# A two-layer decoder trunk on one core: where the down-projection writes four of its norms and one of its weight differences

## The chip, the core and the metric

The kernel runs on one core of a Trainium2 chip. The metric is the device time of one execution in microseconds (us). The engines of the core are TensorE (PE in the profile, PEld for its weight loads), VectorE (DVE), ScalarE (ACT), GpSimd (POOL) and SyncE (SP, which here only issues DMAs). The kernel before takes 2775.11 us, the median of three runs (2769.86 to 2777.68).

## The reference, cut to what matters

The trunk has two layers (DEPTH = 2) on 1024 tokens of 1024 features, all in float32. What concerns the change is the end of each layer, where `h = silu(a) * b` has 2816 features:

```
ffn = jnp.einsum('bsf,fd->bsd', jax.nn.silu(a) * b, w_down)
return layer_norm(ALPHA * x + ffn, ln2_g, ln2_b)
```

The layer norm takes mean and variance over the 1024 features of a token, divides by `sqrt(var + 1e-5)`, multiplies by the gain `g` and adds `b`.

## The kernel before, in words

**Products.** A float32 product is made of three matmuls (lines 110 to 112): each operand is split into a high part (ScalarE, line 90) and the rest (VectorE or GpSimd, line 94), and high x high, high x low and low x high are summed in one PSUM bank. `split` takes an engine for the second part; `L94` in a row is thus the second half of a split, on DVE or on POOL.

**Down-projection.** `down` (line 834 on) uses a 2x2 block scheme with seven products in place of eight. In the order of `plan` they are A11, A12, S2, S1, S4, S3, A22, numbered n = 0 to 6 in the code; the text calls them the first to the seventh product. Each is a sum over 11 steps j (two of the 22 blocks of 128 features per step). In a step, `operands` loads a block of `h` from DRAM (line 860) and up to two 128x512 blocks of `w_down`, forms a sum or difference of weights, and splits block and weights into 128x1024 parts; then PE does four quarters q (one PSUM bank each), three matmuls a quarter, so 12 matmuls a step. Four PSUM banks (`bank_a`) hold one set of sums and four (`bank_x`) another. After a product's last step, `add` (lines 903 to 907) adds banks to the rows `y` of the result, 128 tokens each: tiles 0, 2, 4, 6 are complete after the fifth product, tiles 1, 3, 5, 7 after the seventh. The last six steps of the seventh product (eight in the last layer, `LATE`) have operands in buffers of their own, and PE does them quarter by quarter, so that each quarter's tile can be finished while PE does the next (line 933 on).

**Differences of the weights.** The weight operand of the first product is a block itself; that of S2, S1, S3 and A22 is a difference that GpSimd makes. In the third product (S2, lines 872 to 881) a step loads the block of `h`, `w1[:, hi]` and `w0[:, hi]`; GpSimd makes T2 (line 880), which this step's split needs at once, and T3 (line 881), which is kept in `kept` and needed only by the sixth product (S3). In the fourth product (S1) GpSimd makes one more difference a step (line 888), needed by the seventh. The fifth product (S4, line 889) needs no difference: its step loads `h` and `w1[:, hi]`, and one instruction of 1024 columns splits them. `e_lo` (line 893) gives the second half of the splits of the odd steps of the sixth product to GpSimd, all others to VectorE.

**Norms.** `finish` (line 958) norms a finished tile: statistics of two halves (`bn_stats`, line 259), aggregation (267), a square root on ScalarE (269), reciprocal and a correction of it (271 to 277, instructions of one column), `(z - mean) * g` on VectorE (290), the multiplication by the reciprocal root on ScalarE (291), and the addition of `b` (292), on GpSimd in the first layer and on VectorE in the last. It also appends a piece of work to `pend`: in the first layer the transposition of the tile for the next layer (`to_first`: eight transposes on PE, line 298, then splits), in the last the store of the tile to the output (line 971, issued by SP). `pending()` takes one piece off that list. The even tiles are finished right behind the fifth product.

**Order.** SP and PE run their instructions in the order in which the program writes them. On VectorE, ScalarE and GpSimd a list scheduler of the compiler sets the order at build time: of what is ready by its own clock it takes the instruction of highest priority, which is the one written first, unless a block raises the priority (`urgent`, `high_priority`). On the chip every engine then works strictly in that order. In the text each load stands directly ahead of its use; SP runs ahead of that as far as free buffers let it: the raw blocks go in turn to tags `ws` (3 buffers), `X` (14, shared with what is kept) and `s` (3), the split operands to `w` (6 buffers, two a step, so three steps).

Of the kernel before, what the change touches and what calls it, by code (L numbers as in the profile page):

```python
# [15 lines left out]
ALU = mybir.AluOpType  # L16
# [44 lines left out]
class Trunk:  # L61
# [772 lines left out]
    def down(self, l):  # L834


        nc = self.nc
        last = l + 1 == DEPTH
        wd = self.ins["w_down"]
        lo, hi = slice(0, HALF), slice(HALF, 1024)  # L840
        bank_a = [self.bank() for _ in range(4)]
        bank_x = [self.bank() for _ in range(4)]
        kept, t2 = [None] * NJ, [None] * NJ
        y, half = [None] * 8, [None] * 4
        stages = itertools.cycle(("ws", "X", "s"))
        first = itertools.cycle(("ws", "X", "ws"))

        def operands(n, name, j, late):

            st = self.new([P, 1024], F32, next(first if n == 0 else stages))  # L850
            if late or (n == 0 and j < 4):
                both = self.new([P, 2, 1024], F32R, "X")
                wh, wl = both[:, 0, :], both[:, 1, :]
            else:
                wh, wl = self.new([P, 1024], F32R, "w")[:], self.new([P, 1024], F32R, "w")[:]
            hs = st[:, lo]
            if name == "A11":
                b1 = self.new([P, HALF], F32, "s")
                hs = b1[:]
            nc.sync.dma_start(hs, self.hs[STATIONARY.index(name), j])  # L860
            w0, w1 = wd[l, 2 * j], wd[l, 2 * j + 1]
            other = None
            if name == "A11":

                nc.sync.dma_start(st[:], w0)
                if j % 2 == 0:
                    kept[j] = self.new([P, 2, 2, HALF], F32, "X")
                nc.gpsimd.tensor_tensor(kept[j - j % 2][:, j % 2, 0, :], st[:, hi], st[:, lo], op=ALU.subtract)
                other = st[:, lo]
            elif name == "A12":  # L870
                nc.sync.dma_start(st[:, hi], w1[:, lo])
            elif name == "S2":

                k = kept[j - j % 2][:, j % 2]
                nc.sync.dma_start(st[:, hi], w1[:, hi])
                nc.sync.dma_start(k[:, 1, :], w0[:, hi])
                if j % 4 == 0:
                    t2[j] = self.new([P, 4, HALF], F32, "X")
                other = t2[j - j % 4][:, j % 4]
                nc.gpsimd.tensor_tensor(other, st[:, hi], k[:, 0, :], op=ALU.subtract)  # L880
                nc.gpsimd.tensor_tensor(k[:, 1, :], st[:, hi], k[:, 1, :], op=ALU.subtract)
            elif name in ("S1", "S3"):
                other = kept[j - j % 2][:, j % 2, int(name == "S3"), :]
                if name == "S1":

                    t4 = t2[j - j % 4][:, j % 4]
                    nc.sync.dma_start(st[:, hi], w1[:, lo])
                    nc.gpsimd.tensor_tensor(t4, t4, st[:, hi], op=ALU.subtract)
            elif name == "S4":
                nc.sync.dma_start(st[:, hi], w1[:, hi])  # L890
            else:
                other = t2[j - j % 4][:, j % 4]
            e_lo = "gpsimd" if n == 5 and j % 2 else "vector"
            if other is None:
                self.split(wh, wl, st[:], "scalar", e_lo)
            else:
                self.split(wh[:, lo], wl[:, lo], hs, "scalar", e_lo)
                self.split(wh[:, hi], wl[:, hi], other, "scalar", e_lo)
            return wh, wl

        def add(q, odd, cs, ps, first, op):
            z = y[2 * q + odd][:, cs]
            with self.urgent():
                if first:
                    nc.vector.scalar_tensor_tensor(z, z, ALPHA, ps, op0=ALU.mult, op1=op)  # L905
                else:
                    nc.vector.tensor_tensor(z, z, ps, op=op)

        def step(banks, q, ops, first, end):
            wh, wl = ops  # L910
            ts = slice(q * P, (q + 1) * P)
            self.product(banks[q][:], [(wh[:, ts], wl[:, ts], wh[:, hi], wl[:, hi])], first, end, True)


        plan = [
            ("A11", bank_a, True, False, []),
            ("A12", bank_x, True, True, [(0, lo, False, ALU.add)]),
            ("S2", bank_a, False, False, [(0, hi, True, ALU.add)]),
            ("S1", bank_x, True, False, [(1, hi, True, ALU.add)]),
            ("S4", bank_x, False, True, [(0, hi, False, ALU.add)]),  # L920
            ("S3", bank_a, False, True, [(1, hi, False, ALU.add), (1, lo, True, ALU.add)]),
            ("A22", bank_a, True, True, [(1, lo, False, ALU.subtract)]),
        ]
        for n, (name, banks, fresh, closes, reads) in enumerate(plan):
            if n == 4:
                g, b = self.gains(l, 1)
            held = []
            for j in range(NJ):
                if n == 0 and j == 3:
                    self.flush(True)  # L930
                if not last and (n, j) in ((5, 6), (5, 9), (6, 1), (6, 3)) or last and n == 6 and j in (1, 2, 3, 4):
                    self.pending()
                late = n == 6 and j >= NJ - (LATE if last else 6)
                ops = operands(n, name, j, late)
                if late:
                    held.append((j, ops))
                    continue
                for q in range(4):
                    step(banks, q, ops, fresh and j == 0, closes and j == NJ - 1)
                if n == 1 and j < 8:  # L940
                    y[j] = self.new([P, D], F32, "pt" if j in (0, 1, 2) else "q" if j == 3 else "t")
                    nc.sync.dma_start(y[j][:], self.spill1[j])
                if n == 1 and j == 9:
                    for q in range(4):
                        add(q, 0, lo, bank_a[q][:], True, ALU.add)
            for q in range(4):
                for j, ops in held:
                    step(banks, q, ops, False, j == NJ - 1)
                for odd, cs, first, op in reads:
                    add(q, odd, cs, banks[q][:], first, op)  # L950
                if n == 4:
                    self.finish(l, 2 * q, y, g, b)
                elif n == 5:
                    half[q] = self.stats(y[2 * q + 1], (1,))
                elif n == 6:
                    self.finish(l, 2 * q + 1, y, g, b, self.stats(y[2 * q + 1], (0,), half[q]))
# [144 lines left out]
```

## Time and profile before

| | |
|---|---|
| median of three runs | 2775.11 us (2769.86 to 2777.68) |
| profiled execution | 2775.4 us, span 2773.4 us |
| mean granted TensorE clock | 0.971 |
| busy, share of the span | PE 93%, PEld 76%, DVE 69%, ACT 44%, POOL 53% |
| DMA | 140 GB/s over the span, HBM read 281.75 MB, written 104.43 MB |

The profiled execution's own time is 2.0 us over its span. Matmuls are pipelined: the duration of one in a row is longer than the distance to the next, so steps are read from start times. Idle time in square brackets is that of the engine just before the instruction, with what ended it.

### The profile page before, as it was taken

Reading aid. Unit: us, or ns where it says so; the run is one execution under the profiler, and the core shown is the slowest. Engines: PE = TensorE matmul, PEld = TensorE weight load, DVE = VectorE, ACT = ScalarE, POOL = GpSimd, SP = SyncE. Lnnn points to the kernel's source line nnn. Section 1 sums busy time; section 2 is a strip of 40 time slices with the busy share of each in tenths; the row PEclk is TensorE's granted clock in tenths of the full one; section 3 lists DMA queues with packets and bytes.
Section 4 is the critical chain, followed back from the end, with each engine's and each line's share of the span. In section 5 each row is a group of like instructions: output and inputs, shape, how many; then the busy total and the mean of one; then the engine's idle time right before and its main releaser. Section 6 shows DMA issues by size and latency. Waiting matters only on the chain.

```text
span 2773.4 us, 32010 instructions
## 1 busy us (share of the span) xinstructions
PE 2583.8 (93%) x11408; PEld 2105.9 (76%) x11408; DVE 1919.5 (69%) x2310; ACT 1233.4 (44%) x2050; POOL 1457.2 (53%) x962
## 2 busy tenths in 40 slices
PE   5989999998899999899889999999988999998887
PEld 4868887787688888677667788777867888877676
DVE  6565556737887877786675656477478887767866
ACT  4434445523544554434444444454335455544343
POOL 2554456767466555370434545566674556553701
PEclk8999999999999999999899999999999999999999
DMA  3433358554133333674323423765532333327742
GB/s 123 138 114 107 108 196 225 161 181 150 57 104 114 114 99 107 222 277 134 106 95 117 142 75 108 237 189 164 201 122 75 96 107 103 114 92 266 267 139 76
DMA packets 163232, 389.59 MB, mean 140 GB/s; under 512 B 17408, under 2 KB 48896, under 8 KB 162048
## 3 DMA queue, kind: packets, MB, share of 16 engines
q1 hardware_dynamic: 136496, 293.02, 32.3%
q0 software_dynamic: 14848, 55.09, 7.0%
q10 hardware_dynamic: 11728, 39.45, 3.7%
q8 instruction: 89, 1.46, 0.2%
q14 instruction: 71, 0.58, 0.1%
HBM read 281.75 MB, written 104.43 MB: 139 GB/s over the span
## 4 chain that ended last, share of the span: by engine, by line
PE 49%; DVE 16%; issue 5%; DMA 3%; ACT 3%; POOL 3%; ACTq 0%; DVEq 0%; SPq 0%; POOLq 0%
PE b L111 16%; PE b L112 16%; PE b L110 16%; DVE w L94 3%; DVE X L94 2%; DVE st L259 1%; DVE ve L275 1%; DMA X<-in_w_down 1%; POOL ws L738 1%; DVE pt L811 1%; ACT w L90 1%; POOL w L94 1%; DVE t L290 1%; DMA X<-h_blocks 1%; DVE w L321 0%
## 5 line engine op out<-in xcount | busy, mean ns | idle before, releaser
L110 PE MATMUL b<-X,w 128*128 128x512 f32 x2552 | 1014.1, 397 | 55.1 <-ACT s L727 20.0
L112 PE MATMUL b<-X,w 128*128 128x512 f32 x2552 | 1008.3, 395 | 27.9 <-DVE w L94 18.6
L111 PE MATMUL b<-X,w 128*128 128x512 f32 x2552 | 1006.5, 394 | 3.2 <-DVE X L94 3.2
L94 DVE TENSOR_TENSOR w<-ws,w 128x512 fp32r<-128x512 f32 (+1 forms) x454 | 450.4, 996 | 358.5 <-ACT w L90 346.3
L90 ACT CAST w<-ws 128x512 fp32r<-128x512 f32 (+1 forms) x608 | 408.0, 677 | 489.6 <-PE b L112 154.5
L110 PEld LDWEIGHTS b<-X,w 128*128 128x128 f32 x2552 | 487.4, 191 | 167.5 <-ACT s L727 24.6
L112 PEld LDWEIGHTS b<-X,w 128*128 128x128 f32 x2552 | 486.9, 191 | 136.4 <-DVE w L94 22.5
L94 POOL TENSOR_TENSOR w<-ws,w 128x512 fp32r<-128x512 f32 (+2 forms) x154 | 297.5, 1934 | 532.5 <-ACT w L90 520.3
L111 PEld LDWEIGHTS b<-X,w 128*128 128x128 f32 x2552 | 487.3, 191 | 105.9 <-DVE X L94 5.5
L741 POOL TENSOR_TENSOR ql<-ws 128x512 f32<-128x512 f32 x82 | 125.0, 1524 | 354.8 <-DMA ws<-in_w_in 254.0
L111 PE MATMUL b<-w,w 128*128 128x512 f32 x528 | 214.4, 406 | 48.5 <-DVE w L94 41.3
L110 PE MATMUL b<-w 128*128 128x512 f32 x528 | 211.1, 400 | 2.7 <-DVE pt L905 1.4
L112 PE MATMUL b<-w,w 128*128 128x512 f32 x528 | 210.6, 399 | 0.0
L111 PEld LDWEIGHTS b<-w,w 128*128 128x128 f32 x528 | 102.0, 193 | 82.4 <-DVE w L94 54.3
L738 POOL TENSOR_TENSOR ws<-ws,ws 128x512 f32<-128x512 f32 x82 | 142.4, 1736 | 6.2
L811 DVE SCALAR_TENSOR_TENSOR q<-t,par,q 128x1023 f32<-128x1023 f32 x88 | 127.4, 1448 | 19.0 <-ACT q L808 18.1
L94 DVE TENSOR_TENSOR w<-X,w 128x512 fp32r<-128x512 f32 (+1 forms) x107 | 121.5, 1158 | 22.3 <-ACT w L90 22.3
L738 POOL TENSOR_TENSOR ws<-ql,ws 128x512 f32<-128x512 f32 x82 | 125.0, 1524 | 6.3
L738 POOL TENSOR_TENSOR ws<-ws 128x512 f32<-128x512 f32 x82 | 118.6, 1446 | 16.9 <-DVE w L94 12.7
L110 PEld LDWEIGHTS b<-w 128*128 128x128 f32 x528 | 102.0, 193 | 28.3 <-DVE t L905 2.7
L811 DVE SCALAR_TENSOR_TENSOR pt<-t,par,pt 128x1023 f32<-128x1023 f32 x88 | 123.3, 1401 | 0.2
L112 PEld LDWEIGHTS b<-w,w 128*128 128x128 f32 x528 | 102.1, 193 | 20.6
(242 smaller groups left out, 3783.6 us busy)
## 6 DMA issues: line engine op xcount, KB each, us to landing
ws<-in_w_up SPq DMA_DIRECT2D x88, 512.0 KB
ws<-in_w_in SPq DMA_DIRECT2D x75, 512.0 KB
gates<-t ACTq DMA_DIRECT2D x48, 512.0 KB
ws<-in_w_o SPq DMA_DIRECT2D x40, 512.0 KB
h_blocks<-t SPq DMA_DIRECT2D x80, 256.0 KB
s<-h_blocks SPq DMA_DIRECT2D x66, 256.0 KB
t<-gates SPq DMA_DIRECT2D x32, 512.0 KB
t<-q_parts POOLq DMA_DIRECT2D x64, 256.0 KB, 4.1
```

The lines of the kernel that those rows point to most:

```text
L90: self.nc.scalar.copy(hi, src)
L94: return eng.tensor_tensor(lo, src, hi.bitcast(F32), op=ALU.subtract)
L110: self.nc.tensor.matmul(out, wh, xh, start=start and i == 0, stop=False, skip_group_check=more)
L111: self.nc.tensor.matmul(out, wh, xl, start=False, stop=False, skip_group_check=more)
L112: self.nc.tensor.matmul(out, wl, xh, start=False, stop=stop and i == n - 1, skip_group_check=more)
L259: self.nc.vector.bn_stats(st[:, c, :], z[:, c * HALF:(c + 1) * HALF])
L275: nc.vector.scalar_tensor_tensor(ve[:], ve[:], r[:], r[:], op0=ALU.mult, op1=ALU.mult)
L290: nc.vector.scalar_tensor_tensor(z[:], z[:], mv[:, 0:1], g[:], op0=ALU.subtract, op1=ALU.mult)
L738: sub = lambda out, x, y: nc.gpsimd.tensor_tensor(out, x, y, op=ALU.subtract)
L741: nc.gpsimd.tensor_tensor(s1[:], a21, a22, op=ALU.add)
L811: nc.vector.scalar_tensor_tensor(y[:, d:], c[:, :S - d], w(k), y[:, d:], op0=ALU.mult, op1=ALU.add)
```

## The change

Three things in the down-projection change.

First, the load of `w0[:, hi]` and the GpSimd difference T3 go from the steps of the third product to those of the fifth.

Second, the norms of the even tiles are no longer written behind the fifth product. They are written in the sixth, tile j - 1 ahead of the operands of step j = 1, 3, 5, 7.

Third, in the first layer the first two of the four pending transpositions go from steps 6 and 9 of the sixth product to its steps 8 and 10.

```diff
                 k = kept[j - j % 2][:, j % 2]
                 nc.sync.dma_start(st[:, hi], w1[:, hi])
-                nc.sync.dma_start(k[:, 1, :], w0[:, hi])
                 if j % 4 == 0:
                     t2[j] = self.new([P, 4, HALF], F32, "X")
                 other = t2[j - j % 4][:, j % 4]
                 nc.gpsimd.tensor_tensor(other, st[:, hi], k[:, 0, :], op=ALU.subtract)
-                nc.gpsimd.tensor_tensor(k[:, 1, :], st[:, hi], k[:, 1, :], op=ALU.subtract)
...
             elif name == "S4":
+
+                k = kept[j - j % 2][:, j % 2, 1, :]
                 nc.sync.dma_start(st[:, hi], w1[:, hi])
+                nc.sync.dma_start(k, w0[:, hi])
+                nc.gpsimd.tensor_tensor(k, st[:, hi], k, op=ALU.subtract)
...
-                if not last and (n, j) in ((5, 6), (5, 9), (6, 1), (6, 3)) or last and n == 6 and j in (1, 2, 3, 4):
+                if not last and (n, j) in ((5, 8), (5, 10), (6, 1), (6, 3)) or last and n == 6 and j in (1, 2, 3, 4):
                     self.pending()
+                if n == 5 and j in (1, 3, 5, 7):
+                    self.finish(l, j - 1, y, g, b)
...
-                if n == 4:
-                    self.finish(l, 2 * q, y, g, b)
-                elif n == 5:
+                if n == 5:
                     half[q] = self.stats(y[2 * q + 1], (1,))
```

## Rows read from the trace of the kernel before

**Rows 1.** The page, part 1: busy time of each engine over the span.
```profile
PE 2583.8 (93%) x11408; PEld 2105.9 (76%) x11408; DVE 1919.5 (69%) x2310; ACT 1233.4 (44%) x2050; POOL 1457.2 (53%) x962
```

**Rows 2.** Busy time by stretch (us): PE, PEld, DVE, ACT, POOL; clock, DMA share, GB/s.
```profile
1206.00:1274.30 68.30, 61.63 (x259) 47.43 (x258) 56.83 (x55) 24.54 (x42) 43.69 (x27) 1.00 0.63 215
1274.30:1304.40 30.10, 30.10 (x134) 24.71 (x134) 15.88 (x17) 11.73 (x14) 0.01 (x1) 1.00 0.33 105
2585.70:2654.10 68.40, 61.34 (x256) 46.86 (x255) 56.84 (x56) 24.48 (x42) 44.10 (x27) 1.00 0.63 217
2654.10:2684.10 30.00, 30.00 (x133) 24.70 (x132) 15.85 (x17) 11.68 (x14) 0.00 (x0) 1.00 0.38 122
...
1304.40:1354.80 50.40, 38.12 (x152) 30.48 (x151) 28.28 (x56) 22.76 (x40) 25.00 (x14) 0.83 0.32 110
2684.10:2726.60 42.50, 34.48 (x141) 27.64 (x139) 38.45 (x68) 27.70 (x48) 15.54 (x10) 0.88 0.39 125
2726.60:2747.60 21.00, 16.61 (x61) 12.41 (x62) 10.21 (x18) 1.14 (x2) 0.00 (x0) 0.92 0.00 1
...
2684.10:2736.90 52.80, 40.39 (x159) 31.25 (x158) 48.66 (x84) 28.84 (x50) 15.54 (x10) 0.89 0.31 101
```

**Rows 3.** Timeline of PE, third product, first layer: first waits of two neighbouring steps.
```profile
1227.36 0.50 PE L111 MATMUL b<-w,w 128*128 128x512 f32 x1 [0.39 <-DVE w L94]
...
1230.76 0.50 PE L111 MATMUL b<-w,w 128*128 128x512 f32 x1 [0.38 <-DVE w L94]
```

**Rows 4.** Timeline of POOL and DVE, third and fourth product, first layer.
```profile
1226.72 1.74 POOL L881 TENSOR_TENSOR X<-s,X 128x512 f32<-128x512 f32 x1
1228.42 1.74 POOL L880 TENSOR_TENSOR X<-ws,X 128x512 f32<-128x512 f32 x1
...
1227.23 1.78 DVE L94 TENSOR_TENSOR w<-ws,w 128x512 fp32r<-128x512 f32 x1
...
1252.54 0.69 DVE L94 TENSOR_TENSOR w<-s,w 128x512 fp32r<-128x512 f32 x1
```

**Rows 5.** Timeline of PE, sixth product, first layer, then last layer.
```profile
1317.16 0.79 PE L111 MATMUL b<-w,w 128*128 128x512 f32 x1 [5.12 <-DVE w L94]
1317.75 0.63 PE L112 MATMUL b<-w,w 128*128 128x512 f32 x1
1318.17 0.63 PE L110 MATMUL b<-w 128*128 128x512 f32 x1
...
1329.67 0.80 PE L111 MATMUL b<-w,w 128*128 128x512 f32 x1 [7.16 <-POOL w L94]
...
2699.77 0.79 PE L111 MATMUL b<-w,w 128*128 128x512 f32 x1 [8.02 <-DVE w L94]
```

**Rows 6.** Timeline of POOL and of DVE, start of the sixth product, first layer.
```profile
1314.70 6.98 POOL L292 TENSOR_TENSOR t<-t,t 128x1024 f32<-128x1024 f32 x2 [7.76 <-ACT t L291]
...
1327.13 1.26 POOL L94 TENSOR_TENSOR w<-s,w 128x512 fp32r<-128x512 f32 x1
...
1315.82 1.29 DVE L94 TENSOR_TENSOR w<-X,w 128x512 fp32r<-128x512 f32 x2
```

**Rows 7.** Timeline of PE, sixth product: the eight transposes of one pending tile.
```profile
1340.65 1.03 PE L298 MATMUL b<-ident,pt 128*128 128x128 f32 x8
```

**Rows 8.** Timeline of DVE, SP and ACT: a wide split beside POOL; load and cast of the fifth product.
```profile
1196.75 2.00 DVE L94 TENSOR_TENSOR w<-ws,w 128x1024 fp32r<-128x1024 f32 x1 [1.50 <-ACT w L90]
...
1250.05 0.42 SPq L890 DMA_DIRECT2D ws<-in_w_down  x1
...
1270.92 1.05 ACT L90 CAST w<-ws 128x1024 fp32r<-128x1024 f32 x1 [1.58 <-PE b L112]
```

**Rows 9.** Timeline of DVE, third product: statistics of the norms that are written after the fifth.
```profile
1212.40 0.68 DVE L259 BATCH_NORM_STATS2 st<-pt 128x6 f32<-128x512 f32 x1
```

**Rows 10.** Timeline of DVE, end of the last layer: first and last instruction of one tile.
```profile
2747.62 0.69 DVE L907 TENSOR_TENSOR pt<-pt,b 128x512 f32<-128x512 f32 x1 [10.81 <-PE b L112]
...
2752.59 1.23 DVE L292 TENSOR_TENSOR pt<-pt,t 128x1024 f32<-128x1024 f32 x1 [1.22 <-ACT pt L291]
```

## The prediction

> **What bounds the kernel now.** The page's busy times come first: PE is busy 93% of the span [rows 1], so time can only be won where PE waits. The table of busy time by stretch, cut at the additions that close the products, shows where it waits in the down-projection [rows 2]. The fifth product is the measure of a product without waits: 30.1 us in the first layer, 30.0 in the last, 2.73 us for each of 11 steps. The third and fourth together take 68.3 and 68.4 us, 8.1 and 8.4 over two such products. The sixth takes 50.4 and 42.5.
>
> The timeline says why. In the third product PE waits at every step, and its steps lie 3.40 us apart (1227.36 to 1230.76) [rows 3]. GpSimd's two differences of a step start 1.70 us apart, back to back, so the pair takes exactly the step [rows 4]. VectorE is held by it: its 128x512 split takes 1.78 us there and 0.69 once GpSimd is quiet [rows 4]. The two take turns: one instruction of each costs 1.70 us, of which VectorE's own is 0.69, so GpSimd's share is 1.01.
>
> In the sixth product the waits are few and long: 5.12 us for a split on VectorE, then 7.16 for one on GpSimd, in the first layer, and 8.02 for one on VectorE in the last; behind them matmuls start 0.42 us apart (1317.75, 1318.17) [rows 5]. The granted clock of these stretches is 0.83 and 0.88 [rows 2], so part of each runs at 1.2 GHz in place of 2.4. The cause is the norms: the wide GpSimd additions begin at 1314.70 and the first GpSimd split behind the four of them starts at 1327.13; the VectorE split of step 2 starts at 1315.82, behind the norms' arithmetic [rows 6].
>
> **The change part by part.** *Third and fourth product.* A step of the third loses one GpSimd difference and one load of 256 KB. What is left at the shared place is two VectorE splits and one difference: 2 x 0.69 + 1.01 = 2.4 us, under PE's 2.73. So the excess, 8.1 + 8.4 = 16.5 us, should go. Kept back: 1 us a layer for single collisions where the four closing additions and the early statistics of the norms [rows 9] meet a difference. Gain 14.5; bounds 10 (half of each step's wait survives in the first steps, where GpSimd catches up with loads) and 16.5.
>
> *Fifth product.* Each step gains the load and the difference, 11 a layer. GpSimd is idle there (0.01 and 0.00 us busy [rows 2]), so the difference itself is hidden; so is its effect on VectorE: the wide split with GpSimd beside it took 2.00 us [rows 8], still under 2.73, and a cast is issued as soon as the split buffers of three steps earlier are free. Of the load: SP issues the fifth product's first weight block at 1250.05 and its cast starts at 1270.92 [rows 8], 21 us or seven to eight steps later; one more issue of 0.42 us a step on SP, and the longer hold of the raw buffer until GpSimd has read it, fit there. Behind the waiting difference on GpSimd stand only the next one and, a product later, the odd splits of the sixth. Cost 0, bounds 0 and 4 (a wait of 0.4, like that of rows 3, at each of 11 steps in one layer). If GpSimd falls behind, the raw buffers are late next, and then SP's loads.
>
> *Sixth product, first layer.* Excess now: 50.4 - 30.1 - two tiles' transposes of 1.03 each [rows 7] = 18.2 us, which contains the two waits and the matmuls at half clock behind them. With the norms written between the steps, a split that is ready goes ahead of later tiles' norms, and VectorE and GpSimd meet one norm in two steps instead of four at once. But the shared place fills up. In two steps (5.46 us) VectorE has two splits of 0.69 and one wide multiplication, taken as two such halves, 2.76 in all; GpSimd has two split halves and a wide addition, four times 1.01: 6.8 us. That is 1.3 too much, four times: 5.4. Splits are begun some steps ahead, which swallows about one of the four overruns, so about 4.2 stays, in waits too short for the clock to fall (the waits of 0.4 us in rows 3 left it at 1.00 in rows 2). Gain 14; bounds 8 (double the residue and some half-clock) and 18.
>
> The Trainium skill, on the page "SBUF — State Buffer", section "Who interferes with whom", says that a VectorE instruction with two SBUF inputs and a GpSimd instruction that reads SBUF exclude each other for the whole instruction. By whole durations (0.69 and 1.26 [rows 4, 6]) an alternating pair would take 1.95 us, and the trace shows 1.70, so the turn-taking is there but costs less; by the rule the two steps would take 7.8 us, the residue would be about 7, and the total 3 us higher than mine. I go by the rows.
>
> *Sixth and seventh product, last layer.* The addition of the bias is on VectorE here, and the scheduler also does splits of the seventh product early. Up to the last of these splits VectorE is busy 48.66 of 52.8 us [rows 2]: it is nearly the bound itself, and moving work does not shrink it. Without any wait the seventh product's first closing addition would come 30.0 + 13.6 us after 2684.1 (three full steps of 2.73 and eight quarter steps of 0.68), at 2727.7; now it comes at 2747.6, 19.9 later. VectorE's 48.7 us end at 2732.8 at the earliest, and about 1 us later the addition can come; that allows 13.8. I take 11, for idle VectorE where a norm waits for ScalarE. The stores of the tiles stand between SP's loads of the seventh product and now wait for later norms; the last norm, written at step 7, should end near 2711, and the loads behind it are needed about 10 us on. Bounds 5 and 16, the upper end if less of VectorE's time goes to turn-taking.
>
> *Transpositions moved* by two steps and by one: same work on PE, nobody waits for it before the next layer's first product. Cost 0; uncovered it would be one block, 1 us.
>
> **Sum.** 14.5 + 14 + 11 = 39.5 us off the profiled execution's 2775.4: 2735.9, say 2736. The median is 2775.11, so the two stand level. PE bounds what follows the first layer's down-projection as well (93% busy over the span [rows 1]), so what is won there is kept.
>
> **Rivals.**
>
> *The sixth product keeps most of its wait.* The additions on GpSimd stand in front of the odd splits one after another, and in the last layer VectorE gains nothing from spreading. For it: the 6.8 against 5.46 us, and 48.66 of 52.8. Against: the long waits were single waits behind four norms. Gains 14.5 + 5 + 4: 2752.
>
> *The order doesn't change.* The scheduler takes what is ready; the norms' first statistics run at 1212.40, two products ahead of their place in the text [rows 9]. If all four norms are again placed at once behind the fifth product, only the third product gains: 2761. Against: at that moment the splits now stand earlier in the text than three of the four norms.
>
> *The pace moves with the difference.* The fifth product becomes paced by GpSimd and VectorE as the third was. Only the norms gain, 25 us: 2750. Against: one wide split and one difference are under 2.73 us.
>
> *Slower.* Place: the odd steps of the sixth product. Engines work strictly in order, and one tile's norm alone, with nothing else on the engines, takes 6.2 us from its closing addition to its bias (2747.62 to 2753.82 [rows 10]). If splits stand behind such chains, each of the eight norms makes a stall instead of one or two long ones, and behind each PE falls to half clock. Price: 4.3 us of wait and 12 matmuls 0.2 us longer, 6.7 a norm, 54 us against today's 18.2 + 12.5; with the 14.5 won, about 8 us slower: 2783. It decides where a norm holds a split some 4 us beyond its lead. Against: the chain's gaps are open to splits.
>
> **How the numbers follow.** Forecast 0.68; sixth product keeps its wait 0.14; same order 0.06; pace moves 0.04; slower 0.04; nothing measurable, because a new wait of some other kind takes the gain, 0.04. The sum of best bounds is 16.5 + 18 + 16 = 50.5, 2725; of worst 10 + 8 + 5 - 4 = 19, 2756. With the first and third rival inside and a little room, 2722 to 2758 leaves out about 0.18. A difference of 0.3%, 8 us, is about what a measurement of this kernel can tell from none; all cases but the last two are beyond it: faster 0.92, same 0.04, slower 0.04.
>
> **What would show it.** Right: in the third product one GpSimd difference a step, VectorE splits mostly near 0.69, PE steps 2.73 apart; third and fourth together near 61 us; differences of the fifth product beside a PE that doesn't wait; the sixth product of the first layer near 36 us with a granted clock near 1.00, and no wait over 3 us in it. Wrong: steps still 3.4 us apart anywhere; the four norms again in one block; long waits for GpSimd's odd splits; or a wait of SP at the stores that makes the seventh product's last steps late.

## The result, and the profile after

The changed kernel takes 2750.97 us (median of six runs, 2749.37 to 2755.65), the kernel before 2776.39 in the same comparison. The ratio is 0.9915, 95% interval 0.9901 to 0.9929: faster by 0.85%, some 25 us, inside the stated range, but by about two thirds of the 39.5 us forecast.

The page's first part answers to [rows 1]; PE's busy time is little less, the span is shorter (2749.7 us against 2773.4):

```profile
PE 2578.7 (94%) x11408; PEld 2106.8 (77%) x11408; DVE 1914.2 (70%) x2310; ACT 1232.2 (45%) x2050; POOL 1445.9 (53%) x962
```

The table of busy time by stretch, cut at the same places as [rows 2]. For each layer: third and fourth product, fifth, sixth, seventh up to its first closing addition (us; PE, PEld, DVE, ACT, POOL; clock, DMA share, GB/s).

```profile
1206.30:1267.30 61.00, 59.27 (x259) 48.02 (x258) 46.89 (x55) 24.58 (x42) 34.97 (x24) 1.00 0.70 237
1267.30:1297.30 30.00, 30.00 (x133) 24.70 (x133) 17.48 (x16) 11.69 (x14) 5.18 (x3) 1.00 0.37 123
1297.30:1343.60 46.30, 37.91 (x151) 29.84 (x151) 35.86 (x56) 22.39 (x39) 25.25 (x14) 0.89 0.36 119
1343.60:1370.80 27.20, 23.90 (x103) 18.63 (x102) 22.82 (x36) 11.42 (x22) 7.25 (x5) 0.94 0.22 68
2576.80:2637.90 61.10, 59.31 (x260) 48.08 (x259) 48.36 (x56) 24.61 (x42) 35.96 (x24) 1.00 0.70 237
2637.90:2667.90 30.00, 30.00 (x133) 24.69 (x132) 15.94 (x17) 11.65 (x14) 5.04 (x4) 1.00 0.46 141
2667.90:2702.90 35.00, 32.57 (x141) 25.86 (x139) 34.60 (x60) 22.90 (x40) 15.86 (x10) 1.00 0.46 150
2702.90:2724.00 21.10, 16.94 (x64) 12.40 (x63) 15.07 (x27) 5.40 (x11) 0.00 (x0) 0.92 0.01 3
```

The third and fourth product fell from 68.3 and 68.4 to 61 us, the fifth stayed at 30.0 with GpSimd at work beside it (5.18 and 5.04 us). The sixth fell from 42.5 to 35.0 in the last layer, but only from 50.5 to 46.3 in the first, where the seventh grew from 25.1 to 27.2, by the starts of the closing additions in both traces. Most of the missing 14 us are there.

GpSimd works ahead of PE: while PE is in the third product, it already makes the fourth product's differences (line 886 of the changed kernel). It now idles between them and waits for loads, where it ran back to back in [rows 4], and VectorE's splits in these gaps have their short time. What is left of PE's waits in the third product stands in its first steps (0.33, 0.39 and 1.01 us), among closing additions and statistics (timelines of POOL, DVE and PE):

```profile
1225.35 1.29 POOL L886 TENSOR_TENSOR X<-X,X 128x512 f32<-128x512 f32 x1 [1.57 <-DMA X<-in_w_down]
...
1224.38 0.68 DVE L94 TENSOR_TENSOR w<-X,w 128x512 fp32r<-128x512 f32 x1
...
1220.28 0.50 PE L111 MATMUL b<-w,w 128*128 128x512 f32 x1 [1.01 <-DVE w L94]
```

In the sixth product of the first layer PE still has two places with long waits. The timeline of PE answers to [rows 5]:

```profile
1311.14 0.50 PE L111 MATMUL b<-w,w 128*128 128x512 f32 x1 [0.71 <-DVE ve L276]
...
1319.00 0.75 PE L111 MATMUL b<-w,w 128*128 128x512 f32 x1 [4.83 <-POOL w L94]
...
1328.66 1.04 PE L298 MATMUL b<-ident,pt 128*128 128x128 f32 x8
1330.94 0.49 PE L110 MATMUL b<-w 128*128 128x512 f32 x1 [1.24 <-ACT w L90]
...
1333.54 0.80 PE L112 MATMUL b<-w,w 128*128 128x512 f32 x1 [1.18 <-DVE w L94]
```

The first long wait is read back through three engines (timelines of POOL, ACT and DVE):

```profile
1302.83 1.40 POOL L94 TENSOR_TENSOR w<-s,w 128x512 fp32r<-128x512 f32 x1 [2.94 <-ACT w L90]
...
1306.82 2.99 POOL L292 TENSOR_TENSOR pt<-pt,t 128x1024 f32<-128x1024 f32 x1 [1.34 <-ACT pt L291]
1312.61 2.39 POOL L292 TENSOR_TENSOR pt<-pt,t 128x1024 f32<-128x1024 f32 x1 [2.81 <-ACT pt L291]
1314.95 3.99 POOL L94 TENSOR_TENSOR w<-X,w 128x512 fp32r<-128x512 f32 x2
```

```profile
1311.38 1.16 ACT L291 ACTIVATE pt<-pt,r 128x1024 f32<-128x1024 f32 x1 [3.23 <-DVE r L277]
1312.44 1.13 ACT L90 CAST w<-X 128x512 fp32r<-128x512 f32 x2
...
1325.32 0.60 ACT L90 CAST w<-X 128x512 fp32r<-128x512 f32 x1
...
1329.30 1.07 ACT L90 CAST X<-b 128x512 fp32r<-128x512 f32 x2 [3.38 <-PE b L298]
1330.26 1.15 ACT L90 CAST w<-X 128x512 fp32r<-128x512 f32 x2
```

```profile
1302.99 1.25 DVE L275 SCALAR_TENSOR_TENSOR ve<-ve,r 128x1 f32<-128x1 f32 x1
...
1307.54 2.82 DVE L94 TENSOR_TENSOR w<-ws,w 128x512 fp32r<-128x512 f32 x1
...
1311.20 0.15 DVE L277 TENSOR_TENSOR r<-r,ve 128x1 f32<-128x1 f32 x1
...
1312.89 3.19 DVE L290 SCALAR_TENSOR_TENSOR t<-t,mv,t 128x1024 f32<-128x1024 f32 x1
1316.01 1.21 DVE L277 TENSOR_TENSOR r<-r,ve 128x1 f32<-128x1 f32 x1
```

PE waits for GpSimd's splits (1314.95). In front of them on GpSimd stands a wide addition (1312.61), which waited for ScalarE's multiplication (1311.38), which waited 3.23 us for the last of the one-column instructions of its tile on VectorE (line 277, 1311.20). Most of these 3.23 us is a split in front of them on VectorE: it took 2.82 us (1307.54) beside GpSimd's wide addition for the tile before (1306.82), where a split alone takes 0.68. So the wide additions act twice: they stand in front of GpSimd's splits, and they hold up VectorE's, behind which the next tile's chain waits.

In the chains of other tiles instructions of a single column are long themselves, 1.25 and 1.21 us: the one at 1302.99 ends at 1304.24, just when the GpSimd split that began before it ends (1304.23).

The second place is another chain. ScalarE's high splits of the transposed tile (1329.30) stand in its queue between the two casts of step 8 (1325.32 and 1330.26). They wait for PE's transposes, which the change writes at step 8, so PE does them only after step 7 (1328.66). Step 8's second cast thus can't run ahead of PE, and PE waits for it and the splits behind it.

### The profile page after: what moved, and what is told of

The parts are those of the page before. It is cut to its first block, busy times and chain, and to the rows that moved or that the text cites. A ratio compares the mean times of both kernels' runs of the same rounds, so it can differ in the third digit from the quotient of the medians.

```text
span 2749.7 us, 32031 instructions
## 1 busy us (share of the span) xinstructions
PE 2578.7 (94%) x11408; PEld 2106.8 (77%) x11408; DVE 1914.2 (70%) x2310; ACT 1232.2 (45%) x2050; POOL 1445.9 (53%) x962
## 5 line engine op out<-in xcount | busy, mean ns | idle before, releaser
L110 PE MATMUL b<-X,w 128*128 128x512 f32 x2552 | 1013.8, 397 | 55.9 <-ACT s L727 18.9
L94 DVE TENSOR_TENSOR w<-X,w 128x512 fp32r<-128x512 f32 (+1 forms) x107 | 108.7, 1035 | 23.9 <-ACT w L90 22.3
```

What stands on the lines that cost most here:

```text
L94: return eng.tensor_tensor(lo, src, hi.bitcast(F32), op=ALU.subtract)
L110: self.nc.tensor.matmul(out, wh, xh, start=start and i == 0, stop=False, skip_group_check=more)
```

## The experiments

All stretches below are measured as above, between the starts of the first closing additions, in the profiled execution (us). "3+4" is the third and fourth product together. The experiments were measured in three groups, each with the kernel before beside it; its medians were 2777.90 (first four experiments of the table), 2775.71 (next four) and 2777.34 (last four), so ratios are compared, not medians. A stretch can move without being touched: e3 changes only the first layer, and its last layer's seventh product is 1.6 us shorter. Differences of that size in one stretch say little.

| kernel | first layer 3+4, 5, 6, 7 | last layer 3+4, 5, 6, 7 | median us | ratio to before (95%) |
|---|---|---|---|---|
| before | 68.3, 30.1, 50.5, 25.1 | 68.4, 30.0, 42.5, 21.1 | | |
| changed | 61.0, 30.0, 46.3, 27.2 | 61.0, 30.0, 35.0, 21.1 | 2750.97 | 0.9915 (0.9901 to 0.9929) |
| e1_difference_only | 61.0, 30.1, 49.0, 26.7 | 61.0, 31.0, 42.6, 21.1 | 2767.37 | 0.9958 (0.9942 to 0.9975) |
| e2_norms_only | 68.3, 30.0, 46.1, 27.2 | 68.3, 30.0, 35.0, 21.1 | 2765.66 | 0.9954 (0.9937 to 0.9970) |
| e4_transposes_back | 61.0, 30.0, 40.5, 25.1 | 61.0, 30.1, 35.0, 20.8 | 2748.63 | 0.9888 (0.9871 to 0.9906) |
| e6_one_instruction | 59.1, 30.6, 43.2, 25.6 | 61.0, 30.0, 37.3, 21.1 | 2750.53 | 0.9896 (0.9879 to 0.9912) |
| e3_bias_on_vector | 61.0, 30.9, 41.8, 27.2 | 61.0, 30.0, 35.0, 19.5 | 2744.52 | 0.9886 (0.9871 to 0.9900) |
| e5_one_input | 61.1, 30.4, 44.2, 25.7 | 61.0, 30.1, 34.0, 20.9 | 2741.69 | 0.9873 (0.9858 to 0.9888) |
| e7_odd_splits_on_vector | 61.0, 31.6, 42.5, 25.6 | 61.1, 31.4, 30.6, 18.9 | 2742.70 | 0.9876 (0.9861 to 0.9891) |
| e8_one_instruction_one_input | 61.2, 30.0, 39.6, 25.7 | 61.0, 30.0, 35.8, 19.5 | 2737.39 | 0.9863 (0.9847 to 0.9880) |
| c1_back_odd_on_vector | 61.0, 31.6, 40.2, 25.7 | 61.0, 30.6, 30.6, 20.5 | 2740.71 | 0.9873 (0.9854 to 0.9891) |
| c2_back_odd_one_input | 61.1, 31.0, 39.1, 25.7 | 61.1, 31.5, 32.1, 20.8 | 2737.91 | 0.9857 (0.9841 to 0.9873) |
| c3_back_bias_one_input | 61.0, 30.0, 33.5, 26.7 | 61.1, 30.0, 34.0, 21.1 | 2730.77 | 0.9828 (0.9808 to 0.9848) |
| c4_back_fused_first_odd_last | 59.2, 30.0, 38.8, 27.3 | 61.1, 31.1, 32.1, 21.1 | 2737.51 | 0.9858 (0.9842 to 0.9875) |

**The parts by themselves.** The first run keeps only the difference in the fifth product (`finish` behind n == 4 and the transpositions at `(5, 6), (5, 9)`, as before).

> The changed kernel with its second and third part undone: T3 is made in the fifth product, the norms of the even tiles stand behind the fifth product as before, the transpositions at steps 6 and 9. If the parts add up: third and fourth product together 61 us in either layer (changed kernel 61.0 and 61.1, before 68.3 and 68.4), sixth product 50 and 42.5 us as before, in all about 14 us under the kernel before, 2762. If instead the relief of the third product only counts together with the moved norms, the sixth product should come out longer than 50 us or the total above 2768.

The third and fourth product take 61.0 us in both layers, as expected. The sixth is about as before: in the first layer 1.5 us less, which the seventh gives back. The last layer's fifth took 1 us more. The kernel is faster by 0.42%, some 12 us (7 to 16 by the interval) where 14 were expected.

The second run is the reverse: the kernel before with the norms and the transpositions of the changed one.

> The kernel before with only its norms and transpositions moved as in the changed kernel; T3 stays in the third product. If the parts add up: third and fourth product 68.3 us, sixth product 46 us in the first layer and 35 in the last, seventh product of the first layer 2 us longer than before, in all about 10 us under the kernel before, 2767. If the difference in the fifth product disturbs the sixth, the sixth product of the first layer should be clearly shorter here than 46 us.

It gave 68.3, 46.1 and 35.0 us, as expected: the sixth product is the same with T3 in the third product or in the fifth. 0.42% and 0.46% together are 0.88%, close to the changed kernel's 0.85%: within the intervals the parts add up.

**The transpositions.** The third part of the change undone by itself:

```diff
-                if not last and (n, j) in ((5, 8), (5, 10), (6, 1), (6, 3)) or last and n == 6 and j in (1, 2, 3, 4):
+                if not last and (n, j) in ((5, 6), (5, 9), (6, 1), (6, 3)) or last and n == 6 and j in (1, 2, 3, 4):
```

> The changed kernel with its third part undone: transpositions at steps 6 and 9 of the sixth product. Theory A (ScalarE's casts of the transposed tile stand in its queue ahead of step 8's casts and wait for PE, so the transposition at step 8 makes the wait at 1328.7 to 1333.5): that wait goes or halves, sixth product of the first layer about 42 us, total about 4 us under the changed kernel, 2747. Theory B (the waits come from the norms' chain between VectorE, ScalarE and GpSimd, and whatever stands behind is only where it shows): sixth product within 1.5 us of 46.3, the same wait one or two steps earlier, total 2751.

The busy time of its sixth and seventh product in the first layer, and its only wait of PE over 0.8 us in that sixth product:

```profile
1302.00:1342.50 40.50, 34.95 (x154) 28.28 (x153) 35.83 (x56) 23.25 (x41) 25.18 (x14) 0.96 0.40 135
1342.50:1367.60 25.10, 21.79 (x99) 16.73 (x98) 22.19 (x35) 10.48 (x20) 7.25 (x5) 1.00 0.25 76
```

```profile
1323.67 0.80 PE L111 MATMUL b<-w,w 128*128 128x512 f32 x1 [4.84 <-POOL w L94]
```

Theory A holds: the second place is gone, the first stands as it was (4.84 against 4.83 us). The sixth product is 5.8 us shorter, the seventh 2.1, together 7.9, where 4 were expected; the whole kernel's ratio fell by 0.0027 (7.5 us), though the two intervals overlap a little. The part of the change that was priced at nothing costs more than the norms win in the last layer (7.5 us). At step 6 the casts of the tile wait for nobody, since ScalarE comes to them after PE's transposes.

**One instruction for multiplication and bias.** For the even tiles:

```diff
+        if last == "fused":
+            nc.vector.scalar_tensor_tensor(z[:], z[:], r[:], b[:], op0=ALU.mult, op1=ALU.add)
+            return
         nc.scalar.mul(z[:], z[:], r[:])
         getattr(nc, last).tensor_tensor(z[:], z[:], b[:], op=ALU.add)
```

> The changed kernel, but the multiplication by the reciprocal root (ScalarE) and the addition of the bias (GpSimd in the first layer, VectorE in the last) of the even tiles become one VectorE instruction of 1024 columns. It takes away ScalarE's wait for the reciprocal root and GpSimd's wide additions; VectorE gets 1.2 us a tile more in the first layer, nothing more in the last. If ScalarE's in-order wait and the wide additions on GpSimd make the waits: sixth product of the first layer 35 to 38 us in place of 46.3, of the last 33 in place of 35.0, total about 10 us under the changed kernel, 2741. If the shared place of VectorE and GpSimd is simply full, as the prediction's 6.8 against 5.46 us had it: first layer above 42, total above 2747.

Both were missed: the sixth product took 43.2 and 37.3 us. In the first layer PE's wait for GpSimd is gone, but a wait of 3.48 us for a split on VectorE has come, behind the norms' arithmetic there, and the place at step 8 is as it was (PE waits 1.24, 0.41 and 1.18 us). Of ScalarE's waits in this sixth product the second largest is for the transposes at step 8 (waiting for whom, us in total, times, longest):

```profile
ACT w L90 <- PE b L112: 11.0, 4, 4.9
ACT X L90 <- PE b L301: 9.9, 1, 9.9
```

Why the last layer got 2.3 us longer was not followed up.

**Bias on VectorE.** In the first layer, for the even tiles:

```diff
-                self.norm(z, g, b, "vector" if t == 7 else "gpsimd", st)
+                self.norm(z, g, b, "vector" if t == 7 or t % 2 == 0 else "gpsimd", st)
```

> The changed kernel, but in the first layer the bias of the even tiles is added by VectorE, as the last layer does it; the multiplication stays on ScalarE. If GpSimd's wide additions in front of its odd splits, and in front of VectorE's instructions, make the waits: sixth product of the first layer about 37 us (the last layer's 35.0 and 2 for transposes), total 2742. If ScalarE's wait for the reciprocal root makes them: above 41, and ScalarE still waits over 10 us for line 277 in that product.

41.8 us, with 10.1 us of ScalarE's waits for line 277 (12.9 in the changed kernel), just meets the second expectation. But PE's wait of 4.83 us for GpSimd is gone, with 1.70 us for a split on VectorE in its place, and the place at step 8 remains, so this run alone doesn't decide.

**One tensor input in the one-column instructions.**

```diff
-        nc.vector.scalar_tensor_tensor(ve[:], ve[:], r[:], r[:], op0=ALU.mult, op1=ALU.mult)
+        nc.vector.tensor_scalar(ve[:], ve[:], r[:], r[:], op0=ALU.mult, op1=ALU.mult)
...
-        nc.vector.tensor_tensor(r[:], r[:], ve[:], op=ALU.mult)
+        nc.vector.tensor_scalar(r[:], r[:], ve[:], None, op0=ALU.mult)
```

> The changed kernel, but the two one-column instructions of a norm with two tensor inputs (lines 275 and 277) take their second input as a scalar of the instruction. In the changed kernel they take 1.0 to 1.25 us when GpSimd is at work and 0.14 to 0.22 when not, while the one-column instructions with one tensor input (271, 274, 276) always take 0.13 to 0.16. If two tensor inputs are what makes VectorE wait for GpSimd: all of them under 0.3 us, ScalarE's wait for the reciprocal root in the sixth product of the first layer falls from 12.9 to 9 us or less, that product from 46.3 to 44 or less, total 2748. If any VectorE instruction waits: durations and total as in the changed kernel.

The groups of these lines in the sixth product of the first layer (four tiles; busy us, mean ns), first the changed kernel:

```profile
L275 DVE SCALAR_TENSOR_TENSOR ve<-ve,r 128x1 f32<-128x1 f32 x4 | 2.7, 678 | 0.0
L277 DVE TENSOR_TENSOR r<-r,ve 128x1 f32<-128x1 f32 x4 | 2.5, 631 | 0.0
L271 DVE RECIPROCAL r<-sd 128x1 f32<-128x1 f32 x4 | 0.6, 150 | 0.0
```

and then this run:

```profile
L275 DVE TENSOR_SCALAR ve<-ve,r 128x1 f32<-128x1 f32 x4 | 1.1, 268 | 0.0
L277 DVE TENSOR_SCALAR r<-r,ve 128x1 f32<-128x1 f32 x4 | 0.8, 209 | 0.0
L271 DVE RECIPROCAL r<-sd 128x1 f32<-128x1 f32 x4 | 0.6, 155 | 0.1
```

Only the two groups whose inputs changed got shorter, so it is the two tensor inputs that make these instructions wait. ScalarE's waits for line 277 fall from 12.9 to 6.7 us, the sixth product to 44.2, the seventh by 1.5, the last layer's sixth by 1.0. PE's long wait for GpSimd in the sixth product of the first layer stays, at 4.77 us, and so does the place at step 8 (1.24, 0.41 and 1.19). The one-column instructions are thus not what makes these two waits. The split in front of that long wait still takes 2.70 us beside a wide addition of 2.40:

```profile
1308.82 2.40 POOL L292 TENSOR_TENSOR pt<-pt,t 128x1024 f32<-128x1024 f32 x1 [1.11 <-ACT pt L291]
...
1309.06 2.70 DVE L94 TENSOR_TENSOR w<-ws,w 128x512 fp32r<-128x512 f32 x1
```

The total falls by more (0.9873 against 0.9915): the same helper makes all other norms of the kernel too, though what they gained was not read one by one.

**Odd splits on VectorE.** `e_lo = "vector"` in every step:

> The changed kernel, but VectorE also does the second half of the odd steps' splits in the sixth product, so that GpSimd has only the first layer's wide additions there. If splits queued behind wide additions on GpSimd make the waits: sixth product of the first layer 40 us or less. In the last layer GpSimd then does nothing in the sixth product and VectorE gets 6 us more: 35.0 us becomes 37 to 41 if VectorE's load bounds it, and stays at 35 if the waits there came from taking turns with GpSimd.

The sixth product took 42.5 us in the first layer, above what was expected, and 30.6 in the last, below both expectations. The last layer's fifth, sixth and seventh product:

```profile
2636.40:2667.80 31.40, 30.82 (x136) 25.20 (x136) 19.25 (x18) 12.17 (x14) 4.28 (x4) 1.00 0.44 134
2667.80:2698.40 30.60, 30.52 (x134) 24.55 (x133) 30.42 (x65) 20.62 (x34) 0.00 (x0) 1.00 0.36 119
2698.40:2717.30 18.90, 16.50 (x68) 12.11 (x67) 17.49 (x31) 8.01 (x15) 0.00 (x0) 1.00 0.25 87
```

VectorE has ten splits, some 6 us, more to do, and PE doesn't wait in the sixth product. There VectorE is busy 30.42 us instead of 34.60, but part of its work has moved into the stretches beside. Over all three it is busy 67.2 us instead of 65.6 (15.94, 34.60 and 15.07 in the changed kernel): 1.6 us more for some 6 us more work. So some 4 us of what the changed kernel's rows count as VectorE's busy time was waiting for GpSimd. Of the 4.4 us won in the sixth product 1.4 are lost again, because the fifth product's closing addition comes that much later (1.6 in the first layer).

**Both edits of the norm.** One instruction, and scalar inputs:

> Both edits together: multiplication and bias of the even tiles in one VectorE instruction, and the one-column instructions with a scalar as second input. If either wait is the cause by itself, this comes out like the better of the two within 2 us; if they are two terms of one chain, it is lower than either: sixth product of the first layer 34 to 36 us, total 2738 to 2741.

39.6 us is lower than either (43.2 and 44.2), and the total is about as expected, though the first layer's stretch is not. The place at step 8 is still there (PE waits 2.18 us for a cast).

**Together.** Four combinations, all with the transpositions back.

> The changed kernel with its transpositions back at steps 6 and 9 and the odd steps' splits of the sixth product on VectorE. With the transpositions back one long wait is left in the sixth product of the first layer, 4.84 us for a GpSimd split queued behind a wide addition. If that queue is the whole of it: no wait over 3 us there, sixth product of the first layer 36 to 37 us (40.5 with the transpositions back alone), of the last 31 and its seventh to the first closing addition 19, in all about 36 us under the kernel before. If VectorE then becomes the bound in the first layer: 39 us or more there.

40.2 us, against 40.5 with the transpositions back alone, meets the second expectation: GpSimd's queue was not the whole of the first wait. PE now waits for VectorE there:

```profile
PE b L111 <- DVE w L94: 2.7, 1, 2.7
PE b L112 <- DVE w L94: 1.7, 1, 1.7
```

> As the run above, and the one-column instructions of lines 275 and 277 with a scalar as second input. If waits of VectorE for GpSimd in these small instructions still lengthen ScalarE's waits: another 1 to 3 us less in the sixth product of the first layer. If, with no wait left that stops PE, they are off the path: equal to the run above within 1 us.

The sixth product takes 1.1 us less in the first layer, but 1.5 more in the last. By the ratios (0.9857 and 0.9873, intervals overlapping) the two kernels are not told apart.

> Transpositions back, the bias of the first layer's even tiles on VectorE, the one-column instructions with a scalar as second input; odd splits stay on GpSimd. If wide additions ahead of odd splits on GpSimd make the one wait that is left: sixth product of the first layer 35 to 37 us; last layer as with the scalar inputs alone (34.0 and 20.9); in all about 34 us under the kernel before.

The edit is the three diffs above for transpositions, bias and one-column instructions.

```profile
1297.10:1330.70 33.60, 32.97 (x154) 27.08 (x153) 31.81 (x61) 23.34 (x40) 14.79 (x10) 1.00 0.48 165
```

```profile
1317.29 0.50 PE L111 MATMUL b<-w,w 128*128 128x512 f32 x1 [0.63 <-DVE w L94]
```

By the starts of the closing additions this is 33.5 us, less than expected and 1.4 over a product without waits and two transposed tiles, at full clock, and no wait over 0.63 us. With odd splits still on GpSimd and the bias off it, the wait is gone; with the bias on GpSimd and the splits off it (the two runs above) it isn't. So, with the one-column instructions shortened, it is the wide additions on GpSimd that make the rest of the wait, and not the queue of odd splits. No run has the bias on VectorE and the transpositions back without the shortened instructions, so their share in this is open. This kernel is the fastest of all: 2730.77 us, ratio 0.9828 (0.9808 to 0.9848) to the kernel before, some 47 us under it where 34 were expected.

> Transpositions back, scalar inputs, in the first layer multiplication and bias of the even tiles in one VectorE instruction (odd splits on GpSimd), in the last layer the odd splits on VectorE. Puts together what was best in each layer: sixth product 34 to 36 us in the first layer, 31 in the last, in all about 38 us under the kernel before, the lowest of all if the parts add up.

38.8 and 32.1 us are higher than expected: the parts don't add up here. In this kernel's order ScalarE again holds step 8's operands. ScalarE waits 2.11 us for VectorE's fused instruction of a tile before it comes to these casts, and PE waits 1.74 us for one of them:

```profile
1323.38 1.14 ACT L90 CAST w<-X 128x512 fp32r<-128x512 f32 x2 [2.11 <-DVE t L292]
```

That every edit makes the scheduler set a new order may be the reason why parts don't add up; what it did in the last layer was not read.

## Why the prediction was right and wrong

*Third and fourth product: right.* 14.5 us were forecast; 68.3 + 68.4 became 61.0 + 61.0 (14.6 us before rounding), and the first experiment shows it alone. The 1 us a layer that was kept back is there too: 61.0 against two products of 30.0.

*Fifth product: right.* There is no cost: it takes 30.0 us in both layers. The difference is less beside it than was thought, though: GpSimd runs ahead, and in the first layer eight of its eleven differences for the fifth product (line 892 of the changed kernel) are made beside the fourth, between 1248.08 and 1266.05. There the prediction's other sum holds, 2.4 us a step under PE's 2.73.

*Transpositions: the step that failed.* "... same work on PE, nobody waits for it before the next layer's first product. Cost 0; uncovered it would be one block, 1 us." PE's work was counted, the casts of the transposed tile on ScalarE were not. They have raised priority in the program, stand ahead of a cast of step 8, and wait for PE to come to the place where the transposes are written. Undoing that part alone gave back 7.9 us of the first layer's sixth and seventh product.

*Sixth product, first layer: mechanism right, size off.* With the transpositions at their old steps the norms between the steps win 75.5 - 65.6 = 9.9 us of the sixth and seventh product, against 14 forecast; with the transpositions of the change 2.1. The missing 4 are in one wait of 4.84 us and the matmuls at half clock behind it (granted clock 0.96 over that stretch). The term that was mis-sized is "so about 4.2 stays, in waits too short for the clock to fall". It added up each engine's columns, GpSimd's as 1.01 us a half, and spread the excess over the steps. The rows show it gathered in one chain instead: a wide addition on GpSimd holds up a split on VectorE (2.82 us in place of 0.68), the reciprocal root behind it, ScalarE's multiplication (3.23 us of wait) and the next wide addition, and in the queue behind that stand two of PE's splits. Without wide additions on GpSimd (and with short one-column instructions) 33.5 us and no wait over 0.63 were left.

The one-column instructions were put at nothing. The rows show that such an instruction with two tensor inputs waits for the whole GpSimd instruction (1.25 us for 0.2); with scalar inputs the sixth and seventh product of the first layer took 3.6 us less, but the long wait stayed. The Trainium skill ("SBUF — State Buffer", "Who interferes with whom") has both halves of this: one instruction excludes the other for its whole length, and a VectorE instruction with at most one SBUF input, outside the two-port modes, doesn't take part; the scalar inputs (678 and 631 ns to 268 and 209) agree. By its whole durations the residue was put at about 7 us, nearer to the 40.5 - 30.1 - 2.1 = 8.3 that were measured than the 4.2 taken from rows. That nearness is in part luck: the 8.3 contain matmuls at half clock, which neither sum has.

*Last layer: 7.5 us instead of 11.* The gain was taken as 11 of the 13.8 us that VectorE's busy time would allow; 2.8 for an idle VectorE was too little, it was 6.3. The reason was given as "VectorE is busy 48.66 of 52.8 us [rows 2]: it is nearly the bound itself, and moving work does not shrink it." With some 6 us more of splits on VectorE, by which that bound would be near 56 us, the sixth and seventh product up to the first closing addition took 49.5 us, 50.9 with what the fifth gave back, against 56.1 in the changed kernel, and PE didn't wait in the sixth. The busy time held waits for GpSimd; it was no bound.

*The rivals.* The time that came, 2750.97, lies between the third rival's 2750 and the first one's 2752. The third, the moved pace, is ruled out by the fifth product, which doesn't wait. The first, that the sixth product keeps most of its wait, is right in what it says of the first layer: the wide additions do stand in front of the odd splits, and the sign "long waits for GpSimd's odd splits" came (4.83 us). Its sum fits by luck: it had gains of 5 and 4 us in the two layers, and 2.1 and 7.5 came. About 8 us of the first layer's loss came by a mechanism that wasn't among the rivals, the moved transpositions. The same order and the slower case didn't come either: the splits of steps 2 and 3 now run between the norms, and there is no stall per norm.

## What to carry to other kernels

When work is moved on one engine, list all that its helper issues on the others, and ask for each queue whether it now meets an instruction that waits for the moved engine's place. Such an instruction, placed early in an in-order queue, turns a delay that nobody waits for into one that all behind it wait for. In this kernel its raised priority probably put it there; no run took the priority away.

Where VectorE and GpSimd take turns, count instructions, not columns: a correction of one column with two tensor inputs can take as long as GpSimd's instruction beside it (1.25 us beside 1.40), and so can a short split beside a wide addition (2.82 beside 2.99). Then follow who waits behind the one that was held up. And read VectorE's busy time beside GpSimd as an upper bound of its work.

## What the runs showed that was not expected

Giving VectorE more to do made the kernel faster: with some 6 us more of splits VectorE's busy time in the last layer's fifth to seventh product rose by only 1.6 us, from 65.6 to 67.2, and the three took 80.9 us instead of 86.1.

The clock also fell without one long wait: in the changed kernel three waits of 1.24, 0.42 and 1.18 us followed within 3 us, and the matmuls behind them start 0.43 us apart, until 1339.25. The granted clock of that stretch is 0.50, the lower level, 1.2 GHz:

```profile
1334.13 0.63 PE L110 MATMUL b<-w 128*128 128x512 f32 x1
1334.56 0.63 PE L111 MATMUL b<-w,w 128*128 128x512 f32 x1
...
1338.83 0.63 PE L112 MATMUL b<-w,w 128*128 128x512 f32 x1
1339.25 0.54 PE L110 MATMUL b<-w 128*128 128x512 f32 x1
```

```profile
1333.60:1339.20 5.60, 5.60 (x13) 4.45 (x14) 3.11 (x4) 0.99 (x2) 1.02 (x1) 0.50 0.45 145
```

In the third product of the kernel before, waits of 0.39 every 3.4 us left it at 1.00 [rows 2, 3].
